# Loads given out one piece ahead, and branch B's q and k transposed by DMA, in a fused streaming-encoder layer

## The chip, the cores and the metric

The kernel runs on one core of a Trainium2 chip. The time is that of one execution on the device, in microseconds (us), as a median of several executions. Names of engines are those of the profile: PE is TensorE (PEld its weight loads), DVE is VectorE, ACT is ScalarE, POOL is GpSimd, SP is SyncE, whose queue gives out nearly all DMAs.

## The reference, cut to what matters

One layer of an encoder over 2048 prompt frames and 8 x 16 sample frames that continue running streams with 512 cached positions. All in float32; the kernel splits operands into a high and a low fp16 part and multiplies three of the four pairs.

```python
h = rms_norm(x, norm_g) * (1 + scale) + shift            # scale, shift, gate from c @ w_ada + b_ada
qa, ka, va, za, qb, kb, vb, zb, ga, gb = split(h @ w_in)  # 4*512 + 4*512 + 2*1024 columns
# branch A, 4 heads: differential attention, chunk-causal (64), after rope
w  = softmax(q1 k1^T / 8) - lam * softmax(q2 k2^T / 8);   oa = w @ va
# branch B, 8 heads: stick-breaking attention, strictly causal, no rope
z = qb kb^T / 8
a = exp(log_sigmoid(z) + reverse_cumsum(log_sigmoid(-z)) - log_sigmoid(-z));   ob = a @ vb
# merge
ya = (rms_norm(oa, subln_g) * (1 - lam_init) * silu(za)) @ w_branch_a
yb = (ob * silu(zb)) @ w_branch_b
y  = rms_norm(x + gate * ((sigmoid(ga) * ya + sigmoid(gb) * yb) @ w_out), final_g)
```

The outputs are y for prompt and samples and the new k and v of both branches.

## The kernel before, in words

The frames are cut into 17 tiles of 128: tiles 0 to 15 are the prompt, tile `NT` = 16 holds all samples. The program has three stages.

**Prologue** (lines 955 to 1182). The modulation is computed from `w_ada`, x is normalised, modulated, transposed by TensorE and kept in DRAM as `hT_d` in two fp16 halves.

**Units** (lines 891 to 1322). Eight units, each a pair of a head group and a branch: unit u has branch A for even u (`kind` 0, one head of A) and branch B for odd u (`kind` 1, two heads of B). For each unit, `project` multiplies a tile of h with 512 columns of `w_in` (24 matmuls at L438; odd units add 24 gate matmuls at L514 with their own columns). `finish` splits v, k and q into halves on ACT and DVE (`k16`, `qbuf`; L299, L304, L472, L473). `transpose_qk` then turns k (2 blocks of 128x128) and q (4 blocks) with six TensorE transposes (L527, L531) into one PSUM bank `ps_t`, the only bank of its tag, which the gate matmuls use too; two copies (L541, L542) bring them to `k` and `qst`, on ACT in A units and on DVE in B units. `scores` multiplies q with all earlier k (L649, L650, three `ps_s` banks). In A units DVE evacuates (L568) and ACT exponentiates; in B units ACT makes two sigmoids (L123), DVE scans (L626), POOL multiplies (L632), ACT casts (L582), DVE makes the low half (L583). In both, the weights are transposed by a DMA (L590, `wt`, up to 16 blocks of 128x128 each), and `pv`, two steps later (`PV_LAG`), multiplies them with v (L706 to L711).

Projections form one long list of pieces over all units, which runs some tiles ahead of the attention (`LEAD`, `take`); `interleave` mixes pieces of projection, scores and pv of one step by their costs. `transpose_qk` of a tile stands in that list five pieces after the start of the next tile's projection (`TR_AFTER`). Side work is spread over the steps: `prepare_unit` loads the next unit's 512 columns of `w_in` (and gate columns), squares them on ACT for a scale (`norm`, L281, junk output), then cuts them into halves; `norms().one` loads `w_branch`, `w_out` and the value caches and squares them likewise; the key caches go through `stages`, which already fetches one piece before it squares. Buffers of 4 KB per partition come from one list, `free`, first in, first out. The order of instructions on each engine is made by the framework's own scheduler from this program; each engine then runs its list strictly in order. On SP that means: a DMA that waits for its data holds up every DMA behind it.

**Last stage** (from L1322 on). For each tile, `inputs` loads o, z and the two gates (`g_d`, L1222), makes u = o * silu(z), takes the gates' sigmoid (L1236), squares and splits u; `turned` transposes u on TensorE (L1209); `branches` multiplies with `w_branch` (L1366) and the gates (L1368); `turned_y`, `output` (L1395) and `normed_rows` follow. `inputs` runs two tiles ahead, `turned` one tile ahead. The eight units' sample attention (`sample`, tiles `dsc`, `dks`, `dwt`) is mixed in.

## Time and profile before

| what | value |
| --- | --- |
| median of 3 executions (lowest, highest) | 2332.06 us (2321.65, 2335.35) |
| the profiled execution, its span | 2326.12 us, 2324.3 us |
| busy: PE, DVE, ACT, POOL | 2096.5, 1745.0, 1621.7, 704.5 us |
| DMA: queue of SP | 76.4% of 16 engines' span, 442 MB |
| granted PE clock, mean | 0.969 |

By stage, from the first score of a unit to that of the next (start, length): prologue 0, 134 us; unit 0 134, 183 us; unit 1 (B) 317, 233 us; unit 2 550, 194 us; unit 3 (B) 744, 241 us; unit 4 985, 188 us; unit 5 (B) 1173, 251 us; unit 6 1424, 182 us; unit 7 (B) 1606, 214 us; last stage 1820, 504 us. Tiles are numbered from 0, so tile 8 of unit 3 is the ninth prompt tile of the second B unit.

In the tables of stretches, each row gives the stretch and its length in us, then for each engine the busy time and the number of instructions, then the granted PE clock (1.00 is full), the DMA share and GB/s. In rows of groups, "x64 | 26.4, 413 | 0.0" is 64 instructions, 26.4 us busy, 413 ns each in the mean, 0.0 us idle ahead of them.

### The profile page before, as it was taken

The numbers are of one execution on the slowest core, as the hardware profiler recorded it, in microseconds if no ns is written. First come the engines' busy times: TensorE is split into PE (matmuls) and PEld (weight loads), VectorE is DVE, ScalarE is ACT, GpSimd is POOL, SyncE is SP. The second block draws the span as 40 slices with busy tenths as digits, with TensorE's granted clock in tenths as the row PEclk, the third lists the DMA queues.
The fourth block names the chain that finished last, engine by engine and source line by source line (L and its number), as shares of the span: only waits on it lengthen the run. The fifth ranks groups of instructions, "written<-read, shape, count | busy, mean of one in ns | idle before, by whom it ended". The sixth has DMA issues, their size and how long they took to land. (4 is left out here: it accounts for less than half of the span.)

```text
span 2324.3 us, 41797 instructions
## 1 busy us (share of the span) xinstructions
PE 2096.5 (90%) x14752; PEld 1123.2 (48%) x14752; DVE 1745.0 (75%) x3795; ACT 1621.7 (70%) x3228; POOL 704.5 (30%) x610
## 2 busy tenths in 40 slices
PE   5998899998989889899998998999998689899998
PEld 3654454444545445455554444555454344444443
DVE  4658668789776777997767879787778878777763
ACT  4968676788776677878676887776677666556541
POOL 1223014356410433752023346401345312122111
PEclk7999999999999999999999999999999799999999
DMA  9778558889696798878877898665667899778421
GB/s 335 272 213 212 134 146 220 198 198 184 174 239 150 201 231 186 187 184 220 183 200 206 182 221 199 171 156 138 142 157 165 191 273 256 211 219 215 143 100 52
DMA packets 805827, 445.30 MB, mean 192 GB/s; under 512 B 537354, under 2 KB 744506, under 8 KB 805104
## 3 DMA queue, kind: packets, MB, share of 16 engines
q1 hardware_dynamic: 804668, 442.24, 76.4%
q8 instruction: 115, 1.88, 0.3%
q14 instruction: 96, 0.79, 0.1%
q10 hardware_dynamic: 948, 0.39, 0.1%
HBM read 228.82 MB, written 86.02 MB: 135 GB/s over the span
## 5 line engine op out<-in xcount | busy, mean ns | idle before, releaser
L632 POOL TENSOR_TENSOR sc_p<-sc_p,sc_n 128x127 f32<-128x127 f32 (+7 forms) x192 | 311.8, 1628 | 660.2 <-DVE sc_n L626 562.8
L438 PEld LDWEIGHTS <-hs 128*128 128x128 f16 x3120 | 276.5, 99 | 263.3 <-issue 11.9
L438 PE MATMUL ps_mm<-wa,hs 128*128 128x512 f16 x1590 | 400.4, 382 | 2.9 <-DMA hs<-hT_d 2.1
L438 PE MATMUL ps_mm<-wb,hs 128*128 128x512 f16 x1530 | 394.5, 384 | 7.6 <-DMA hs<-hT_d 6.8
L626 DVE TENSOR_TENSOR_SCAN sc_n<-ps_s,sc_n,zero_t 128x512 f32<-128x512 f32 x192 | 245.4, 1278 | 72.2 <-ACT ps_s L123 67.3
L649 PE MATMUL ps_s<-k,qst 128*128 128x512 f16 (+3 forms) x640 | 226.0, 354 | 49.2 <-DVE sc_n L626 38.5
L583 DVE TENSOR_TENSOR sc_n<-sc_p,sc_n 128x128 f16<-128x128 f32 (+7 forms) x192 | 222.7, 1163 | 36.8 <-ACT sc_n L582 36.4
L514 PEld LDWEIGHTS <-hs 128*128 128x128 f16 x1632 | 156.5, 98 | 189.1 <-ACT qst L542 5.9
L123 ACT ACTIVATE sc_p<-ps_s,usc 128x512 f32<-128x512 f32 (+3 forms) x320 | 205.1, 641 | 32.5 <-PE ps_s L650 23.3
L650 PE MATMUL ps_s<-k,qst 128*128 128x512 f16 (+3 forms) x640 | 225.7, 354 | 0.0
L514 PE MATMUL ps_t<-wb,hs 128*128 128x512 f16 x918 | 216.1, 379 | 3.0 <-DVE sam L542 1.4
L710 PE MATMUL ps_o<-v,wt 128*128 128x128 f16 x1088 | 168.9, 225 | 43.1 <-DMA wt<-sc_n 42.7
L123 ACT ACTIVATE ps_s<-ps_s,usc 128x512 f32<-128x512 f32 (+3 forms) x328 | 200.5, 611 | 0.0
L582 ACT CAST sc_n<-sc_p 128x128 f16<-128x128 f32 (+7 forms) x192 | 155.2, 811 | 63.7 <-POOL sc_p L632 62.8
L1395 PE MATMUL ps_o<-wo,wb 128*128 128x512 f16 x816 | 185.2, 382 | 6.3 <-ACT wo L299 5.5
L514 PE MATMUL ps_t<-wa,hs 128*128 128x512 f16 x714 | 170.6, 381 | 6.9 <-ACT qst L542 5.7
L710 PEld LDWEIGHTS <-wt 128*128 128x128 f16 x1088 | 105.0, 101 | 104.7 <-DMA wt<-sc_n 54.6
L711 PE MATMUL ps_o<-v,wt 128*128 128x64 f16 x1088 | 154.5, 198 | 0.0
L568 DVE TENSOR_SCALAR_CACHE_REDUCE sc_n<-ps_s,usc 128x512 f32<-128x512 f32 (+3 forms) x160 | 106.2, 664 | 35.2 <-PE ps_s L650 17.2
L1366 PEld LDWEIGHTS <-wb 128*128 128x128 f16 x816 | 79.2, 100 | 105.5 <-issue 23.1
L711 PEld LDWEIGHTS <-wt 128*128 128x128 f16 x1088 | 102.9, 100 | 50.9 <-issue 2.2
L1395 PEld LDWEIGHTS <-wb 128*128 128x128 f16 x816 | 78.7, 98 | 100.4 <-issue 9.1
(370 smaller groups left out, 4515.6 us busy)
## 6 DMA issues: line engine op xcount, KB each, us to landing
hs<-hT_d SPq DMA_DIRECT2D x130, 512.0 KB, 4.6
g_d<-gt SPq DMA_DIRECT2D x68, 256.0 KB, 4.3
out_dram<-pr SPq DMA_DIRECT2D x204, 64.0 KB, 2.2
wa<-g_d SPq DMA_DIRECT2D x25, 512.0 KB, 3.8
o_d<-o SPq DMA_DIRECT2D x136, 64.0 KB, 2.6
hs<-o_d SPq DMA_DIRECT2D x17, 512.0 KB, 3.8
out_dram<-x SPq DMA_DIRECT2D x17, 512.0 KB, 2.8
wide<-in_w_ada_dram SPq DMA_DIRECT2D x8, 1024.0 KB
```

Source lines behind the costliest of these rows:

```text
L123: i = S.activation(**kw)
L438: T.matmul(box["p"], box["h"][:, hi, k, :], U["w"][k][:, wi, :], start=(n == 0), stop=(n == 3 * KT - 1))
L514: T.matmul(box["g"][:, 0:gw], box["h"][:, hi, k, :], U["wg"][k // per][:, k % per, wi, :], start=(j == 0), stop=(j == 3 * KT - 1))
L582: S.copy(out=hi, in_=src)
L583: V.tensor_tensor(out=lo, in0=src, in1=hi, op=ALU.subtract)
L626: V.tensor_tensor_scan(out=dst[:, lo : lo + n][:, ::-1], data0=src[:, 0:n][:, ::-1], data1=zero_t[:, 0:1].to_broadcast([P, n]), initial=fi ...
L632: G.tensor_tensor(out=p[:, 0:m], in0=p[:, 0:m], in1=n[:, 1 : m + 1], op=ALU.mult)
L649: T.matmul(p[:, 0:n], qst[:, c, :], kk[:, c, 0:n], start=True, stop=False)
L650: T.matmul(p[:, 0:n], qst[:, 2 + c, :], kk[:, c, 0:n], start=False, stop=not diag)
L710: T.matmul(po[:, c * P : (c + 1) * P], wt[:, wj, :], vt[:, c, :, :], start=first, stop=False)
L711: T.matmul(po[:, c * P : c * P + 64], wt[:, nb + wj, :], vt[:, c, 0, :], start=False, stop=last)
L1395: T.matmul(po, st["y"][:, yi * 8 + k, :], wo[j * 4 + k // 2][:, wi, k % 2, :], start=(n == 0), stop=(n == 3 * KT - 1))
```

## The change

Five edits.

1. `prepare_unit`: the loads of the next unit's weights and gate columns are given out one piece ahead of their squares (`staged`), in one piece more.
2. `norms().one`: the same for `w_branch`, `w_out` and the value caches.
3. Prologue: five early pieces where there were four, since unit 0's weights now have five.
4. `transpose_qk`: in B units (`kind` 1) k and q go by two DMA transposes from SP straight from `k16` and `qbuf` to `k` and `qst`. Six TensorE transposes, the PSUM bank and two DVE copies of each of their 4 x 17 tiles are gone. A units stay as they were.
5. Last stage: the gates' sigmoid leaves `inputs` for a piece of its own, `opened`, at the end of the step before its tile.

```diff
         def norm(name, k, i):
...
-            fetch(name, k)
             sum_squares(raw[name, k], 1024, U[name + "acc"][:, i : i + 1])
+
+        def staged(name, ks):
+            def piece(i):
+                if i < len(ks):
+                    fetch(name, ks[i])
+                if i > 0:
+                    norm(name, ks[i - 1], i - 1)
+            return [lambda i=i: piece(i) for i in range(len(ks) + 1)]
...
-        pieces = [lambda k=k: norm("w", k, k // 2) for k in range(0, KT, 2)] + [bounds] + [lambda k=k: cut(k) for k in range(0, KT, 2)]
+        pieces = staged("w", list(range(0, KT, 2))) + [bounds] + [lambda k=k: cut(k) for k in range(0, KT, 2)]
...
     def transpose_qk(U, t):
...
+        if U["kind"] == 1:
+            turned_to = nc.sync.dma_start_transpose
+            turned_to(out=kst, in_=k16.rearrange("p c f d -> p (c f d)"))
+            turned_to(out=qst, in_=q16.rearrange("p f c r d -> p (f c r d)"))
+        else:
+            pt = bank("t", F16)
...
-        def one(src, dst, scale):
-            st = free.pop(0)
-            free.append(st)
-            load(out=st if len(src.shape) == 2 else st.rearrange("p (j n) -> p j n", n=P), in_=src)
-            sum_squares(st, 1024, dst, scale=scale)
+        loaded = []
+
+        def one(k):
+            if loaded:
+                st, dst, scale = loaded.pop(0)
+                sum_squares(st, 1024, dst, scale=scale)
+                free.append(st)
+            if k < len(srcs):
+                src, dst, scale = srcs[k]
+                st = free.pop(0)
+                load(out=st if len(src.shape) == 2 else st.rearrange("p (j n) -> p j n", n=P), in_=src)
+                loaded.append((st, dst, scale))
...
-        for fn in early[0:4]:
+        for fn in early[0:5]:
...
-        for g in gs:
-            act(out=g, in_=g, func=AF.Sigmoid)
-
...
+    def opened(st):
+
+        for g in st["g"]:
+            act(out=g, in_=g, func=AF.Sigmoid)
...
                 work.insert(2, (0.9, lambda n=n: turned(states[tiles[n + 1]])))
+                work.append((0.1, lambda n=n: opened(states[tiles[n + 1]])))
```

The scheduler makes the lists of all engines anew. Three places show it; lines of the changed kernel are numbered up to 23 higher (L438 is L445, L590 is L602, L649 and L650 are L661 and L662, the new k and q transposes are L542 and L543).

First the list of PE at the projection of tile 9 of unit 3, at the point where the six transposes of tile 8 stood (`hs` is the projected tile's h, `wb`, `wa` the unit's weights). Before:

```order
L438 MATMUL ps_mm<-wb_1430,hs_181 128x512
L527 LDWEIGHTS k_9812
L527 MATMUL ps_t<-id_192,k_9812 128x128
L527 LDWEIGHTS k_9812
L527 MATMUL ps_t<-id_192,k_9812 128x128
L531 LDWEIGHTS qbuf_214
L531 MATMUL ps_t<-id_192,qbuf_214 128x128
L531 LDWEIGHTS qbuf_214
L531 MATMUL ps_t<-id_192,qbuf_214 128x128
L531 LDWEIGHTS qbuf_214
L531 MATMUL ps_t<-id_192,qbuf_214 128x128
L531 LDWEIGHTS qbuf_214
```

In the changed kernel, after as many projection matmuls:

```order
L445 LDWEIGHTS hs_181
L445 MATMUL ps_mm<-wa_172,hs_181 128x512
L445 LDWEIGHTS hs_181
L445 MATMUL ps_mm<-wa_172,hs_181 128x512
L445 LDWEIGHTS hs_181
L445 MATMUL ps_mm<-wa_172,hs_181 128x512
L661 LDWEIGHTS qst
L661 MATMUL ps_s<-k,qst 128x512
L662 LDWEIGHTS qst
L662 MATMUL ps_s<-k,qst 128x512
```

The transposes are gone, and the scores of tile 8 have moved up: their first matmul stood behind 1512 projection matmuls of the whole list, and now stands behind 1488.

Second the list of SP around the weights of tiles 7 and 8 of the same unit (`wt` is a transpose of weights, 16 or 2 blocks wide here; `hs` the load of h for a projection; `g_d`, `o_d` and `out` are stores, `in_cache` loads of the spread side work). Before:

```order
L590 DMA_TRANSPOSE wt<-sc_n 128x16x128 x2
L494 DMA out_dram<-pr 128x128
L495 DMA out_dram<-pr 128x128
L700 DMA o_d_68<-o 128x128
L847 DMA wb_1433<-in_cache_a_v_dram 128x8x128
L847 DMA wb_1432<-in_cache_a_v_dram 128x8x128
L590 DMA_TRANSPOSE wt<-sc_n 128x2x128
L415 DMA hs_181<-hT_d_60 128x2048
L518 DMA g_d_105<-gt_1421 128x512
L847 DMA wb_1433<-in_cache_a_v_dram 128x8x128
L847 DMA wb_1432<-in_cache_a_v_dram 128x8x128
L590 DMA_TRANSPOSE wt<-sc_n 128x16x128
```

In the changed kernel:

```order
L602 DMA_TRANSPOSE wt<-sc_n 128x16x128 x2
L602 DMA_TRANSPOSE wt<-sc_n 128x2x128
L525 DMA g_d_105<-gt_1421 128x512
L542 DMA_TRANSPOSE k<-k_9965 128x2x128
L543 DMA_TRANSPOSE qst<-qbuf_214 128x4x128
L602 DMA_TRANSPOSE wt<-sc_n 128x16x128
L602 DMA_TRANSPOSE wt<-sc_n 128x2x128
L501 DMA out_dram<-pr 128x128
L502 DMA out_dram<-pr 128x128
L712 DMA o_d_68<-o 128x128
L525 DMA g_d_106<-gt_1421 128x512
L422 DMA hs_181<-hT_d_60 128x2048
```

k and q of tile 9 now stand behind the first weights of tile 8 and ahead of the rest of them; the load of h, which stood right behind the 2-block transpose, comes nine rows later.

Third the list of ACT in the last stage, at one tile's `inputs` (`hs_181` is z, `hs_180` o, `usq` the square of u, `hs_182` u's split, `wb`, `wa` the gates, `dsc` a sample's scores, L1210 the copy of a transposed u). Before:

```order
L281 ACTIVATE junk,usq<-hs_180 128x1024
L123 ACTIVATE wb_1433<-wb_1433 128x1024
L1372 CAST wa_173<-wa_171 128x512
L299 ACTIVATE hs_182<-hs_180,suy 128x1024
L123 ACTIVATE wa_171<-wa_171 128x1024
```

In the changed kernel:

```order
L281 ACTIVATE junk,usq<-hs_180 128x1024
L123 ACTIVATE hs_181<-hs_181 128x512
L123 ACTIVATE wb_1426<-wb_1426 128x1024
L299 ACTIVATE hs_182<-hs_180,suy 128x1024
L1229 COPY wa_171<-ps_s 128x1024
L123 ACTIVATE wb_1429<-wb_1429 128x1024
```

The two sigmoids on gates still stand near the split of u, but they belong to a tile whose gates were loaded a step earlier.

More of the change, by code (lines that the diff above doesn't have):

```diff
@@ L539, in transpose_qk @@
             kst = U["k"][g][:, :, i * P : (i + 1) * P]
-        copy = V.tensor_copy if U["kind"] == 1 else S.copy
-        copy(out=kst, in_=pt[:, 0:256].rearrange("p (c n) -> p c n", c=2))
-        copy(out=qst, in_=pt[:, 256:768].rearrange("p (j n) -> p j n", j=4))
+        if U["kind"] == 1:
[4 more added lines that the diff above has]
+            pt = bank("t", F16)
+            for c in range(2):
+                T.transpose(pt[:, c * P : (c + 1) * P], k16[:, c, :, :].rearrange("p f d -> p (f d)"), id16)
+            for f in range(2):
+                for c in range(2):
+                    j = 2 + f * 2 + c
+                    T.transpose(pt[:, j * P : (j + 1) * P], q16[:, f, c, :, :].rearrange("p r d -> p (r d)"), id16)
+            copy = V.tensor_copy if U["kind"] == 1 else S.copy
+            copy(out=kst, in_=pt[:, 0:256].rearrange("p (c n) -> p c n", c=2))
+            copy(out=qst, in_=pt[:, 256:768].rearrange("p (j n) -> p j n", j=4))
         if t == NT:
@@ L1285, in first @@
                 turned(states[t])
+                opened(states[t])
         def rest():
```

13 lines of the change are left out of this document (3 added, 10 removed).

## The prediction

> **What bounds the kernel now.** I read the page's first part, then the stretches by stage, then the waits.
>
> ```profile
> PE 2096.5 (90%) x14752; PEld 1123.2 (48%) x14752; DVE 1745.0 (75%) x3795; ACT 1621.7 (70%) x3228; POOL 704.5 (30%) x610
> ...
> 550.00:744.00 194.00, 181.03 (x1308) 100.05 (x1309) 150.95 (x407) 144.38 (x322) 51.95 (x53) 0.99 0.81 191
> 744.00:985.00 241.00, 217.29 (x1501) 114.98 (x1499) 188.35 (x309) 185.08 (x382) 108.00 (x84) 0.98 0.85 200
> ...
> 1606.00:1820.00 214.00, 192.14 (x1362) 102.97 (x1360) 172.88 (x273) 160.09 (x321) 90.77 (x66) 0.96 0.69 153
> 1820.00:2324.00 504.00, 444.64 (x3166) 218.79 (x3164) 353.26 (x788) 267.38 (x366) 97.62 (x67) 0.95 0.69 186
> ```
>
> PE is busy 90 to 93% of every stage of units, DVE and ACT about 78% in unit 3 (744 to 985). An average hides two kinds of stretch:
>
> ```profile
> 784.00:804.00 20.00, 15.28 (x74) 7.15 (x72) 12.65 (x28) 10.27 (x23) 7.41 (x7) 0.74 0.73 191
> 964.00:984.00 20.00, 17.39 (x163) 10.38 (x163) 19.72 (x23) 17.77 (x34) 14.80 (x12) 1.00 0.83 179
> 1666.00:1686.00 20.00, 20.00 (x134) 10.32 (x133) 12.93 (x18) 14.20 (x28) 5.66 (x4) 1.00 0.70 152
> ```
>
> The middle of a B unit is PE's own (20.00 of 20.00); its last tiles are DVE's (19.72). The first row is what a stall does: PE waits, the granted clock falls to 0.74, and 74 matmuls start where the third row has 134. The waits behind it:
>
> ```profile
> PE ps_o L710 <- DMA wt<-sc_n: 42.7, 29, 4.9
> PE ps_s L649 <- DVE sc_n L626: 38.5, 45, 3.4
> ...
> PE ps_o L706 <- DMA wt<-sc_n: 20.8, 19, 2.6
> ...
> PE ps_s L1209 <- DVE dsc L626: 17.7, 5, 5.7
> ```
>
> Each is a late link of the same chain: PE's scores, ACT's sigmoids, DVE's scan (which frees the `ps_s` bank), POOL's product, and the weights that a DMA transposes for pv. L710 is pv of B units, L706 of A units, the last row the samples in the last stage.
>
> **The change part by part.** All sums stand against the profiled execution, 2326.1 us (span 2324.3), which is 5.9 below the median of 2332.1.
>
> *Six transposes off PE.* In an A unit, where the same six stand, PE's rows are:
>
> ```profile
> 599.83 0.28 PE L527 MATMUL ps_t<-id,k 128*128 128x128 f16 x2
> 599.95 0.39 PE L531 MATMUL ps_t<-id,qbuf 128*128 128x128 f16 x4
> 600.17 0.59 PE L438 MATMUL ps_mm<-wa,hs 128*128 128x512 f16 x2
> ```
>
> Durations overlap, so starts count: 600.17 - 599.83 = 0.34 us for six. In B units there are 4 x 17 = 68 tiles: 68 x 0.34 = 23 us. All these transposes come before the DVE stretches at the units' ends, nearly all where PE is the limit: I take -20 (bounds -23 and 0, the latter if other chains end there).
>
> *Waits in front of them.*
>
> ```profile
> L527 PE MATMUL ps_t<-id,k 128*128 128x128 f16 x272 | 38.3, 222 | 17.5 <-DVE k L304 9.0 <-ACT qst L542 4.8 <-ACT gt L517 3.6
> L514 PE MATMUL ps_t<-wb,hs 128*128 128x512 f16 x918 | 216.1, 379 | 3.0 <-DVE sam L542 1.4 <-DVE qst L542 1.0 <-DVE csc L867 0.5
> L514 PE MATMUL ps_t<-wa,hs 128*128 128x512 f16 x714 | 170.6, 381 | 6.9 <-ACT qst L542 5.7 <-DVE sam L542 1.2
> ```
>
> Of the 17.5 us the parts released by `k L304` and by ACT's `qst` are A units' and stay. What goes with B's use of `ps_t`: 3.6 (gate copy) + 1.4 + 1.0 + 1.2 = 7.2 us. I take -6 (0 to -7).
>
> *DVE's copies.*
>
> ```profile
> L542 DVE COPY qst<-ps_t 128x512 f16<-128x512 f16 x64 | 26.4, 413 | 0.0
> L541 DVE COPY k<-ps_t 128x256 f16<-128x256 f16 x64 | 17.7, 276 | 5.8 <-PE ps_t L531 5.7
> ```
>
> 0.69 us a tile, 47 us in all off DVE. It pays only where PE waits for the scan (38.5 us above), mostly at the units' ends, where no copies stood. -3 (0 to -10).
>
> *Loads ahead of their squares.*
>
> ```profile
> L281 ACT ACTIVATE junk<-wa 128x1024 f16<-128x1024 f32 x68 | 72.0, 1059 | 45.7 <-DMA wa<-in_x_prompt_dram 11.1 <-DMA wa<-in_cache_b_k_dram 9.1 <-DMA wa<-in_w_in_dram 7.0
> L281 ACT ACTIVATE junk<-wb 128x1024 f16<-128x1024 f32 x56 | 59.4, 1061 | 39.6 <-DMA wb<-in_w_in_dram 13.8 <-DMA wb<-in_cache_a_v_dram 11.0 <-PE ps_s L220 5.1
> ```
>
> ACT stands up to 85 us ahead of squares; x and the key caches were not changed, so some 50 go. ACT's sigmoids feed the scan, so a few of the 38.5 us of PE's waits end sooner: -5 (0 to -15). The five early prologue pieces do the four's work; the first 79 rows of SP's list are unchanged: 0.
>
> *Gates' sigmoid.*
>
> ```profile
> L123 ACT ACTIVATE wa<-wa 128x1024 f32<-128x1024 f32 x25 | 26.3, 1056 | 50.0 <-DMA wa<-g_d 50.0
> ...
> 601.44 4.05 PE L438 MATMUL ps_mm<-wb,hs 128*128 128x512 f16 x18
> ```
>
> ACT loses 50.0 us to `g_d` at these 25 sigmoids alone. But in the last stage it is busy only 267 of 504 us, and the largest piece of PE's 59 idle ones is the 17.7 behind the samples' scans. A shorter ACT queue feeds those scans earlier: -4 (0 to -15). If a late `opened` put two sigmoids of 1.06 us ahead of L1368, the cover is two `ps_mm` groups of 12 matmuls at 4.05 / 18 = 0.22 us, over 5 us; without it, 2 us for each of 17 tiles.
>
> *What it adds: 136 DMA transposes on SP.* Nothing of 2 or 4 blocks from `k16` exists; the nearest are the weights' transposes, of 2 to 16 blocks.
>
> ```profile
> L590 SPq DMA_TRANSPOSE wt<-sc_n x288: 1167/1746/5657, 147.3 to 1830.6; - x144
> ...
> DMA to landing us min/median/max: 2.3/4.3/6.8
> ```
>
> The smallest issue takes 1.17 us. At 1.2, two a tile are 2.4, and 136 are 163 us of SP's time. How full is SP? The first and last of its 167 issues in unit 3's stretch:
>
> ```profile
> 743.94 0.38 SPq L700 DMA_DIRECT2D o_d<-o  x1
> ...
> 984.66 3.36 SPq L590 DMA_TRANSPOSE wt<-sc_n  x1
> ```
>
> They add up to 160 of 241 us; 34 more at 1.2 make 201, or 83%. The DMA engines stand at 0.85 in that stage; its 102 added blocks of 32 KB are 3.3 MB, which at the row's 200 GB/s is 17 us of 241, 0.07 more: in the mean not full. Queued behind each new issue, and behind its wait for DVE, is everything else on SP: h for the next projection, the weights for pv, the stores that free `pr` and `gt`. PE's waits on these stand at 42.7 us (L710) and, for h,
>
> ```profile
> L438 PE MATMUL ps_mm<-wb,hs 128*128 128x512 f16 x1530 | 394.5, 384 | 7.6 <-DMA hs<-hT_d 6.8
> ```
>
> If lateness grew by half, that is 49.5 / 2 = +25. Weights have two steps until pv and h one tile, most of it slack, so I take +6 (0 to +25), nearer the end at which slack holds.
>
> *q later for its scores.* In SP's list of front, q of tile 9 stands behind the 2-block weights of tile 8. In the trace these and the first score of tile 9 are, for units 3 and 5:
>
> ```profile
> 848.30 1.45 SPq L590 DMA_TRANSPOSE wt<-sc_n  x1
> ...
> 857.06 0.27 PE L649 MATMUL ps_s<-k,qst 128*128 128x256 f16 x1
> ...
> 1279.97 6.95 SPq L590 DMA_TRANSPOSE wt<-sc_n  x2
> ...
> 1288.68 0.27 PE L649 MATMUL ps_s<-k,qst 128*128 128x256 f16 x1
> ```
>
> The weights' issue ends at 849.75; k takes 1.2, q lands 2.3 to 4.3 after its start: 853.3 to 855.3, against 857.06. In unit 5: 1286.92 + 1.2 + 2.3 to 4.3 = 1290.4 to 1292.4, against 1288.68, so 2 to 4 us late. The lists also bring such scores forward: 24 projection matmuls less stand ahead of tile 8, at 0.22 us some 5 us of cover. I count two such places in each of the four B units (tiles 9 and 10, in unit 7 tiles 4 and 5) at 1.3 us, between nothing and the 4 us just found: +10 (0 to +32). Scores are not alone behind it: the next projection's matmuls wait on PE too.
>
> Sum: -20 - 6 - 3 - 5 - 4 + 6 + 10 = **-22 us**, to 2304 against the profiled execution; against the median, 2310.
>
> [...] PE's rows give 0.34 / 6 = 57 ns a block, and the two issues that replace a tile's six blocks take SP 2.4 us. [...]
>
> **The rivals.**
>
> *SP's line becomes the bound of the B units (slower).* k and q wait at the head of SP for DVE, weights and h pile up behind, and PE stands at first scores long enough to lose its clock. For it: 83% of SP's time in issue alone, which leaves 40 us a unit for every wait at SP's head. Against: in the middle of unit 7 the DMAs are lighter (0.70) and PE is full. Price: the stretch at 784 falls 60 matmuls short of 134, 60 / 134 x 20 = 9 us. Two more like it in each of four units are 72 us; less the gains of 38 that is +34, 2366 against the median. It decides once q's landing slips some 4 us beyond my count. [...]
>
> *PE does not get the time.* The scan ends each wait anyway: `ps_s` <- L626 grows by what the transposes leave. For it: DVE and ACT at 78% of unit 3 with only 10% of PE left. Against: 20.00 of 20.00 at 1666. Gains of 38 shrink to 16 and are eaten by +16: 2332.
>
> *SP's slack covers all.* Nothing of the +16, and the squares and gates pay at the far ends: -23 - 7 - 6 - 12 - 12 = -60: 2272.
>
> **How the numbers follow.** About 1% (23 us) is what a measurement can tell from no change here, since the three executions spread over 0.6%. My forecast, -8 to -45, has 0.45, of which 0.25 is beyond 1% faster; the full gain 0.2; PE not getting it 0.1; SP as the bound 0.25, all of it beyond 1% slower in the sum. So faster 0.45, same 0.30, slower 0.25. The range leaves out the outer half of the full gain and of SP as the bound: 2268 to 2366. The forecast's own is 2287 to 2324.
>
> **What would show it.** Right: no L527 or L531 in B units, PE's instructions down by 408, busy PE down in 317 to 1820; ACT's waits at L281 for `in_w_in` and `in_cache` and at the gates near nothing. Wrong: `L661 <- DMA qst` or `k` of over 15 us in total; `wt` and `hs` waits over 1.5 times; stretches with a clock under 0.9 in units 1, 3, 5. If the B units' stretches are as long as before with PE idle at the scan, the second rival holds. What could break the forecast is SP's lateness, which I took from slacks of the old order.

## The result, and the profile after

The changed kernel takes 2334.6 us (median of 20; 2329.6 to 2339.6) where the kernel before takes 2329.0 (20 executions; 2321.7 to 2335.5). The ratio is 1.0017, 95% interval 1.0007 to 1.0026: some 4 us slower, nothing a reader would call a change. The forecast was 2310 us, 22 us faster; the time lies in the stated range of 2268 to 2366, but outside that of the likeliest case, 2287 to 2324, and on the other side of no change.

First the profile's first part for the changed kernel, and the answer on span and clock.

```profile
PE 2089.3 (90%) x14344; PEld 1111.3 (48%) x14344; DVE 1695.3 (73%) x3659; ACT 1618.7 (69%) x3228; POOL 693.9 (30%) x610
```

```profile
core 0: 2330.4 us, clock 0.961
```

PE has 408 matmuls less, as forecast, and DVE 50 us less. Yet PE's busy time fell by only 7.2 us (2096.5 to 2089.3). Three numbers of these rows add up to the span, and the rest of this section reads every kernel by them: **idle** is span less PE's busy time; **clock loss** is (1 - granted clock) x span, the time that PE would have saved at full clock if it had been busy throughout (in the changed kernel two score matmuls start 0.21 us apart at 980.88, at clock 1.00, and 0.41 us apart at 982.62, at 0.50); **work** is busy time less clock loss.

| kernel | span | idle | clock loss | work |
| --- | --- | --- | --- | --- |
| before | 2324.3 | 227.8 | 72.1 | 2024.4 |
| changed | 2330.4 | 241.1 | 90.9 | 1998.4 |
| difference | +6.1 | +13.3 | +18.8 | -26.0 |

So the transposes' time did go: 26 us of PE's work. It was given back as 13 us of standing still and 19 us of running at a lower clock. The mean clock is given in steps of 0.001, so each loss is good to about 1 us.

Two cautions go with this table. PE stands idle for a part of the slow stretches; counted over its busy time alone, the clock costs 49 and 68 us and the work is 2047 and 2021 us, the same 26 apart. Counted like that, the work of all kernels below falls into two groups, 2043 to 2047 us with six TensorE transposes a tile and 2020 to 2027 without (e13_actq, 2032, and e18_k_act, which keeps four of six, 2037, aside). And these are single executions: over all of them the mean clock is 0.963 for the changed kernel (0.957 to 0.967) and 0.967 to 0.968 for the kernel before, which makes the clock's part some 11 us, not 19.

Where it stands still, from the chain of waits of the changed kernel (engine, tile and line waiting; what for; us in all, times, longest):

```profile
PE ps_s L661 <- DVE sc_n L638: 57.5, 54, 3.3
PE ps_o L722 <- DMA wt<-sc_n: 37.8, 23, 4.8
PE ps_o L718 <- DMA wt<-sc_n: 22.4, 18, 2.6
PE ps_s L1228 <- DVE dsc L638: 11.5, 2, 6.7
PE ps_mm L445 <- DMA hs<-hT_d: 11.2, 5, 3.7
```

Against 38.5, 42.7, 20.8 and 17.7 us before, in the rows of the prediction, and for h

```profile
PE ps_mm L438 <- DMA hs<-hT_d: 9.0, 5, 3.0
```

The waits that SP's lateness was expected to raise, weights and h, are as they were (71.4 against 72.5 together). The wait for the scan rose by 19 us. And the same stretches as in the prediction, with the last one to the longer span's end:

```profile
744.00:985.00 241.00, 212.92 (x1429) 111.23 (x1428) 180.96 (x288) 189.62 (x395) 105.36 (x84) 0.99 0.91 209
...
1606.00:1820.00 214.00, 191.79 (x1307) 101.55 (x1305) 169.44 (x252) 164.81 (x331) 90.98 (x66) 0.94 0.78 166
1820.00:2330.00 510.00, 448.46 (x3164) 221.20 (x3162) 343.60 (x787) 267.44 (x366) 92.10 (x67) 0.94 0.70 184
```

In unit 3 and unit 7 PE starts 72 and 55 matmuls fewer in the same time, where 102 transposes a unit are gone, and is busy 4.4 and 0.4 us less. DVE is lighter by 7 and 3 us there and ACT fuller by 5. The units end where they ended before: the last score ends at 1816.6 us, against 1816.7. The 6 us that the profiled execution is longer lie in the last stage, 513.8 us against 507.6 from there on, and it transposes no k or q. That stage is no steady ground: with the same 3172 matmuls in all twenty kernels of this text it takes 500 to 517 us. SP's new issues are (duration of one in ns: smallest, median, largest)

```profile
L542 SPq DMA_TRANSPOSE k<-k x64: 1167/1176/2411, 252.6 to 1771.7; - x64
```

```profile
L543 SPq DMA_TRANSPOSE qst<-qbuf x64: 1188/1217/3183, 259.2 to 1773.0; - x64
```

just the 1.2 us that was taken from the weights' transposes. Last, the squares and the gates' sigmoids on ACT:

```profile
L281 ACT ACTIVATE junk<-wa 128x1024 f16<-128x1024 f32 x72 | 76.7, 1066 | 46.5 <-DMA wa<-in_cache_a_k_dram 12.4 <-DMA wa<-in_x_prompt_dram 10.6 <-DMA wa<-in_cache_a_v_dram 8.6
L281 ACT ACTIVATE junk<-wb 128x1024 f16<-128x1024 f32 x52 | 55.2, 1062 | 31.8 <-DMA wb<-in_w_in_dram 12.5 <-DMA wb<-in_cache_b_v_dram 12.2 <-DMA wb<-in_w_out_dram 3.0
...
L123 ACT ACTIVATE wb<-wb 128x1024 f32<-128x1024 f32 x34 | 34.4, 1049 | 9.5 <-DMA wb<-g_d 9.5
```

The gates' waits went, from 65 us, the 50.0 of the prediction's row and the 15.4 of this one, to 10:

```profile
L123 ACT ACTIVATE wb<-wb 128x1024 f32<-128x1024 f32 x9 | 9.5, 1059 | 15.4 <-DMA wb<-g_d 15.4
```

The squares' did not: 85 us before, 78 now. Although their loads are written one piece ahead, they wait as long.

One place shows how this looks. In unit 3, tile 13, the changed kernel has

```profile
917.54 1.53 SPq L331 DMA_DIRECT2D wb<-in_w_in_dram  x2
919.17 3.61 SPq L602 DMA_TRANSPOSE wt<-sc_n  x1
...
924.74 1.06 ACT L281 ACTIVATE junk<-wb 128x1024 f16<-128x1024 f32 x1 [2.83 <-DMA wb<-in_w_in_dram]
...
927.92 1.28 DVE L638 TENSOR_TENSOR_SCAN sc_n<-ps_s,sc_n,zero_t 128x512 f32<-128x512 f32 x1 [0.78 <-ACT ps_s L123]
...
929.26 0.38 PE L661 MATMUL ps_s<-k,qst 128*128 128x512 f16 x1 [3.29 <-DVE sc_n L638]
```

SP issues from 905 to 940 with hardly a gap. ACT stands 2.83 us at a square whose two loads were issued from 917.54 on and landed at 923.2 and 924.6; the sigmoids come behind the square, DVE's scan behind these, and PE stands 3.29 us for the bank that the scan frees. At the same tile before, PE's waits for scans are 0.7 us in all. That gave the first theory. The place itself does not decide it: the loads were on their way some 3 us before ACT came to the square, so what it stood for there is the rest of a transfer of over 5 us. Whether that was late in SP's list or slow in the DMA engines this place does not tell; the loads of this form take 3.9 to 4.0 us in the median of the kernel before.

### The profile page after: what moved, and what is told of

Its sections match the earlier page's. It is cut to its first block, busy times and chain, and to the rows that moved or that the text cites. A ratio compares the mean times of both kernels' runs of the same rounds, so it can differ in the third digit from the quotient of the medians.

```text
span 2330.4 us, 41287 instructions
## 1 busy us (share of the span) xinstructions
PE 2089.3 (90%) x14344; PEld 1111.3 (48%) x14344; DVE 1695.3 (73%) x3659; ACT 1618.7 (69%) x3228; POOL 693.9 (30%) x610
## 5 line engine op out<-in xcount | busy, mean ns | idle before, releaser
L445 PE MATMUL ps_mm<-wb,hs 128*128 128x512 f16 x1734 | 448.6, 385 | 4.6 <-DMA hs<-hT_d 4.6
L445 PEld LDWEIGHTS <-hs 128*128 128x128 f16 x3120 | 275.7, 99 | 263.6 <-DMA hs<-hT_d 12.7
L445 PE MATMUL ps_mm<-wa,hs 128*128 128x512 f16 x1386 | 349.0, 380 | 6.6 <-DMA hs<-hT_d 6.6
L661 PE MATMUL ps_s<-k,qst 128*128 128x512 f16 (+3 forms) x640 | 228.3, 357 | 72.3 <-DVE sc_n L638 57.5
L595 DVE TENSOR_TENSOR sc_n<-sc_p,sc_n 128x128 f16<-128x128 f32 (+7 forms) x192 | 205.7, 1076 | 49.9 <-ACT sc_n L594 49.6
L521 PE MATMUL ps_t<-wb,hs 128*128 128x512 f16 x918 | 232.4, 380 | 0.0
L662 PE MATMUL ps_s<-k,qst 128*128 128x512 f16 (+3 forms) x640 | 228.0, 357 | 0.0
L722 PE MATMUL ps_o<-v,wt 128*128 128x128 f16 x1088 | 193.6, 228 | 37.9 <-DMA wt<-sc_n 37.8
L521 PEld LDWEIGHTS <-hs 128*128 128x128 f16 x1632 | 144.5, 99 | 140.5 <-issue 10.1
L521 PE MATMUL ps_t<-wa,hs 128*128 128x512 f16 x714 | 187.7, 391 | 6.8 <-ACT qst L554 6.0
L1417 PE MATMUL ps_o<-wo,wa 128*128 128x512 f16 x816 | 182.8, 380 | 2.1 <-ACT wo L299 1.3
L723 PE MATMUL ps_o<-v,wt 128*128 128x64 f16 x1088 | 174.9, 200 | 0.0
L580 DVE TENSOR_SCALAR_CACHE_REDUCE sc_p<-ps_s,usc 128x512 f32<-128x512 f32 (+3 forms) x160 | 106.2, 664 | 26.4 <-PE ps_s L662 24.3
L718 PE MATMUL ps_o<-v,wt 128*128 128x128 f16 x544 | 105.0, 225 | 22.8 <-DMA wt<-sc_n 22.4
```

Source lines behind the costliest of these rows:

```text
L445: T.matmul(box["p"], box["h"][:, hi, k, :], U["w"][k][:, wi, :], start=(n == 0), stop=(n == 3 * KT - 1))
L521: T.matmul(box["g"][:, 0:gw], box["h"][:, hi, k, :], U["wg"][k // per][:, k % per, wi, :], start=(j == 0), stop=(j == 3 * KT - 1))
L580: V.tensor_scalar(out=dst[:, lo : lo + n], in0=p[:, 0:n], scalar1=sc_pos, scalar2=None, op0=ALU.mult, op1=ALU.max, accum_out=job["mx"][:, ...
L595: V.tensor_tensor(out=lo, in0=src, in1=hi, op=ALU.subtract)
L661: T.matmul(p[:, 0:n], qst[:, c, :], kk[:, c, 0:n], start=True, stop=False)
L662: T.matmul(p[:, 0:n], qst[:, 2 + c, :], kk[:, c, 0:n], start=False, stop=not diag)
```

## The experiments

**Theory A (the line).** SP's list is nearly full; the 136 new issues delay what stands behind them, and PE gets the delay over several chains. **Theory B.** PE does not get the time: the chain of scans ends its waits anyway, whatever the transposes cost. Further rivals came up on the way: the transfers' traffic, and k and q that arrive late. In the later expectations theory A stands as L, against D, the transfers. All ratios are to the kernel before on the same chip; differences between two kernels are differences of their ratios times 2330 us, with the two intervals combined.

### Which edit: e1_turn, e2_noturn, e11_gates

The kernel before with edit 4 alone:

```diff
-        pt = bank("t", F16)
-        ... six T.transpose, two copies
+        if U["kind"] == 1: two nc.sync.dma_start_transpose (as in the change)
+        else: as before
```

> The kernel before with edit 4 alone (k and q of B units turned by DMA), loads and gates as before. Theory A, SP's line: the 136 issues delay the loads of weight columns, ACT's squares stand behind these loads, and sigmoids, scans and scores behind the squares; without the staged loads this is worse than in the changed kernel: 10 to 25 us slower than before, ACT's waits at L281 in the units above 90 us. Theory B, PE does not get the time: the scans end PE's waits however the transposes are made, and SP is not to blame: within 5 us of before.

Measured: 1.0075 (1.0055 to 1.0096), 17 us slower, as theory A had it. Its sign at the squares is missed: they wait 76 us in the units, not above 90.

The changed kernel without edit 4:

```diff
-        if U["kind"] == 1: two nc.sync.dma_start_transpose
-        else:
+        (all units) six T.transpose into ps_t, two copies
```

> The changed kernel without edit 4 (TensorE transposes and DVE copies as before; loads, prologue and gates as changed). Theory A: 8 to 20 us faster than before, since the loads now come ahead of their squares; ACT's waits for DMA at the squares in the units fall from 70 to under 35 us. Theory B: edits 1, 2, 3 and 5 are worth next to nothing or cost what the changed kernel lost: between 0 and 6 us slower than before.

Measured: 0.9972 (0.9956 to 0.9988), 6 us faster. Its squares wait 42 us for DMAs in the units, where before has 69 and the changed kernel 67. Theory A had 8 to 20 us and waits of under 35 us, so both fall short of it.

The kernel before with edit 5 alone:

```diff
-        for g in gs:
-            act(out=g, in_=g, func=AF.Sigmoid)
+    def opened(st): ...            # called at the end of the step before
```

> The kernel before with edit 5 alone (the gates' sigmoid in a piece of its own at the end of the step before). As predicted: 4 us faster, the 50 us of ACT's waits for the gates near nothing. If the last stage is bound elsewhere, 0 and within 2 us; edits 1 to 3 then carry the 6 us that e2_noturn gained.

Measured: 1.0002 (0.9988 to 1.0015). ACT's waits for the gates are gone, as this group shows (25 sigmoids; 50.0 us idle before them in the kernel before), and the time has not moved:

```profile
L123 ACT ACTIVATE wa<-wa 128x1024 f32<-128x1024 f32 x25 | 25.6, 1049 | 6.7 <-DMA wa<-g_d 6.7
```

So, by difference, edits 1 to 3 carry the 6 us (+-4); edit 5 is worth nothing (+-3); edit 4 costs 17 us (+-5) without the staged loads and 10 us (+-4) with them (1.0017 less 0.9972). That staging is worth more when SP is fuller would fit, but the two hardly differ by more than their intervals.

### What PE's part is worth: e3_unturned, e4_both

The changed kernel with no transposes of either kind in B units:

```diff
-            turned_to(out=kst, in_=k16.rearrange("p c f d -> p (c f d)"))
-            turned_to(out=qst, in_=q16.rearrange("p f c r d -> p (f c r d)"))
+            V.tensor_copy(out=kst, in_=k16.rearrange("p c f d -> p c (f d)"))
+            V.tensor_copy(out=qst, in_=q16.rearrange("p f c r d -> p (f c) (r d)"))
```

> The changed kernel with neither kind of transpose in B units: two DVE copies bring k16 and qbuf to k and qst as they are, so the transposition of k and q of branch B is left out. PE, SP and DMAs are all free of it. Theory A: with SP free too, PE's 23 us are had: 20 to 40 us faster than before. Theory B: within 6 us of the changed kernel (2329 to 2341), PE's waits for the scan L638 at 55 us or more.

Measured: 0.9931 (0.9912 to 0.9950), 16 us faster than before. So B in its pure form falls: with SP out of the way PE does get something. But theory A's 20 to 40 us are not reached either. Counted over PE's busy time, it has 26 us less work than e2_noturn (2020 against 2046), and it is only 10 us faster (+-6; 5.5 us in the profiled executions): there the clock costs 70 us where e2_noturn has 56, and PE is idle for 227.5 us against 220.8.

The changed kernel with the six TensorE transposes kept beside the DMAs, unread:

```diff
+        pt = bank("t", F16)
+        six T.transpose, in all units
         if U["kind"] == 1:
             two DMA transposes
```

> The changed kernel with the six TensorE transposes kept beside the DMAs in B units, their result in PSUM unread: PE has the work of before, SP that of after. Theory A: PE's transposes cost what they cost before, since PE has no idle time to spare: 10 to 25 us slower than the changed kernel. Theory B: within 5 us of the changed kernel, PE's waits for scans shrinking by what the transposes fill.

Measured: 1.0141 (1.0121 to 1.0160), 29 us slower than the changed kernel (+-5), a little more than theory A's 10 to 25. Here PE's transposes and their waits for `ps_t` are worth what they were sized at, 26 us, with SP's part the same on both sides. And e4_both against e2_noturn, which differ by the DMAs in place of DVE's copies, is 39 us (+-6): that is the other side of the account. Against copies (e3_unturned to the changed kernel) the DMA transposes cost 20 us (+-5). So the same 10 us between e2_noturn and the changed kernel can be read as 10 gained and 20 lost, by way of e3_unturned, or as 39 lost and 29 gained, by way of e4_both; which kernel stands in the middle decides.

### Through what: e5_line, e6_plain, e9_bytes, e16_unread

All four are e3_unturned with something added or put in place of the copies, so they have PE's shorter list in common. Like e3_unturned they leave the transposition of branch B's k and q out of what is computed (e16_unread for the prompt only). Six tiny DMAs on SP a tile:

```diff
+            for j in range(3):
+                load(out=tick[0:1, j, 0:32], in_=k16[0:1, j % 2, j // 2, 0:32])
+            for j in range(3):
+                load(out=tick[0:1, 3 + j, 0:32], in_=q16[0:1, j % 2, j // 2, 0, 0:32])
```

> The kernel of e3_unturned (k16 and qbuf copied by DVE, the transposition of branch B's q and k left out) with six tiny DMAs of 64 bytes a tile on SP, which wait for the same k16 and qbuf: some 2.4 us of SP's line a tile and no traffic. Theory L, the line: SP's time and its waits at the head are what the DMA transposes cost, so most of the 20 us between e3_unturned and the changed kernel come back: 10 to 20 us slower than e3_unturned, 2325 to 2340 on a chip where before takes 2333. Theory D, the transfers: their 3.3 MB a unit in 256-byte packets slow the other DMAs, and SP's line is slack: within 5 us of e3_unturned.

Measured: 0.9966 (0.9949 to 0.9982), 8 us slower than e3_unturned (+-6): less than theory L has for the whole price, more than D's nothing.

Plain DMAs in place of the copies:

```diff
-            two V.tensor_copy
+            load(out=kst, in_=k16.rearrange("p c f d -> p c (f d)"))
+            for j in range(2):
+                load(out=qst[:, j::2, :], in_=q16.rearrange("p f c r d -> p (f c) (r d)")[:, j::2, :])
```

> The same, but k and q go by three plain DMAs a tile in 256-byte pieces from k16 and qbuf to k and qst, without DVE copies: the packets and the arrival of the changed kernel, but a shorter issue (some 0.4 us each) and no transposing; the transposition is left out. Theory L: a third to a half of SP's time, so 3 to 10 us slower than e3_unturned. Theory D by bytes: like the changed kernel, 15 to 22 us slower than e3_unturned; by the transposing itself: within 5 us of e3_unturned.

Measured: 0.9999 (0.9984 to 1.0014), 16 us slower than e3_unturned (+-6). That is more than theory L's 3 to 10 us and fits traffic, or data arriving late.

The same traffic, with nobody waiting for it:

```diff
             two V.tensor_copy
+            load(out=spill[:, 0:2, 0:P], in_=k16.rearrange("p c f d -> p c (f d)"))
+            load(out=spill[:, 2:6, 0:P], in_=q16.rearrange("p f c r d -> p (f c) (r d)"))
```

> The kernel of e3_unturned (transposition of branch B's q and k left out) with two plain DMAs a tile from k16 and qbuf to a scratch in DRAM, in the same 768 pieces of 256 bytes that the transposes move, and nobody waits for them. Some 65 us of SP's issue, the whole traffic, no late q or k. Theory L, the line: 4 to 9 us slower than e3_unturned, 0.3 to 0.5 percent faster than before. Theory D, the transfers: 15 to 20 us slower than e3_unturned, within 0.15 percent of before. If q and k arriving late were the price in e6_plain, this comes out below e6_plain by 8 us or more.

Measured: 0.9927 (0.9906 to 0.9948), the time of e3_unturned. Theory D's 15 to 20 us are missed, and so are the 4 to 9 that theory L had for the issues. Traffic costs nothing here, though it ends in DRAM and not in the buffers of k and q, and by this row of its stretches (unit 3) there was plenty: 0.96 of the DMA engines, more than the changed kernel's 0.91.

```profile
744.00:985.00 241.00, 219.16 (x1466) 114.49 (x1465) 194.05 (x314) 191.87 (x397) 112.31 (x88) 0.97 0.96 211
```

The real DMA transposes, unread:

```diff
+            if t < NT:
+                two V.tensor_copy to kst and qst
+                unread = stg.tile([P, 6, P], F16, tag="sam", ...)
+                qst, kst = unread[:, 0:4, :], unread[:, 4:6, :]
             turned_to(out=kst, ...)
             turned_to(out=qst, ...)
```

> The changed kernel's DMA transposes, 136 with the same sources and waits on SP, but for the prompt tiles into a buffer that nobody reads; k and qst come from DVE copies as in e3_unturned (the transposition of branch B's prompt q and k is left out). SP's line and the transfers are those of the changed kernel, and no score waits for a DMA. If the 20 us between e3_unturned and the changed kernel are the line's (what stands behind on SP): 15 us or more slower than e3_unturned, at most 0.05 percent faster than before. If they are the late k and q: within 5 us of e3_unturned, 0.5 to 0.7 percent faster than before. A part each: between.

Measured: 1.0018 (1.0005 to 1.0030): the time of the changed kernel to the digit, though no score of the prompt waits for a DMA. So late k and q are not the price, unless DVE's copies, which e16_unread has and the changed kernel has not, cost as much by chance. PE's waits for scans are 65.8 us, for weights 69.6 and for h 13.0 (first fence), where e3_unturned has 46.3, 66.2 and 4.4 (second fence).

```profile
PE ps_s L666 <- DVE sc_n L643: 65.8, 53, 4.5
PE ps_o L727 <- DMA wt<-sc_n: 41.9, 24, 4.9
PE ps_o L723 <- DMA wt<-sc_n: 27.7, 19, 5.0
PE ps_mm L445 <- DMA hs<-hT_d: 13.0, 5, 3.3
```

```profile
PE ps_s L660 <- DVE sc_n L637: 46.3, 42, 4.8
PE ps_o L721 <- DMA wt<-sc_n: 41.7, 21, 4.0
PE ps_o L717 <- DMA wt<-sc_n: 24.5, 18, 3.4
...
PE ps_mm L445 <- DMA hs<-hT_d: 4.4, 2, 2.7
```

What these four kernels, e3_unturned and the changed one have on SP in the stretches of the B units (939 us together), summed over its rows in the trace: the time of all issues, and the time that SP stood at the head of its list waiting for data or buffers.

| kernel | issues | issue us | waiting at the head us | slower than e3_unturned |
| --- | --- | --- | --- | --- |
| e3_unturned | 623 | 635 | 262 | - |
| e9_bytes | 722 | 711 | 175 | -1 |
| e5_line | 905 | 717 | 152 | +8 |
| e6_plain | 756 | 736 | 151 | +16 |
| e16_unread | 710 | 755 | 128 | +20 |
| changed | 714 | 758 | 132 | +20 |

Taken as SP's slack, the wait at the head orders these kernels: 76 us more of issue cost nothing while 175 us of slack were left; the next 45 us cost 20. That is what theory A has for a queue that fills. It is not shown to be the whole price. e5_line and e6_plain have the same slack and differ by 8 us, and e9_bytes has hardly less issue time than e5_line and does not pay. The table cannot part issue time from something in the transposing itself, since the last two kernels have both; e5_line and e6_plain have no transposing and pay too. And of what the profiled executions of the changed kernel and of e16_unread are longer than e3_unturned's (13 and 23 us), 8 and 11 us lie behind the last score, where no k or q is transposed.

### Over which chain: e10_deep

The loads of weight columns two pieces ahead of their squares:

```diff
-                if i > 0:
-                    norm(name, ks[i - 1], i - 1)
+                if i > 1:
+                    norm(name, ks[i - 2], i - 2)
```

> The changed kernel with the weights' and gate columns' loads two pieces ahead of their squares where there was one. If SP's lateness reaches PE through ACT's squares (their waits for DMA in the units are 66 us, against 42 in e2_noturn), these waits fall and the kernel is 5 to 12 us faster than the changed one. If the squares are beside the path: within 3 us of the changed kernel.

Measured: 0.9992 (0.9979 to 1.0006), 6 us faster than the changed kernel (+-4). But the squares' waits in the units did not fall (77 us against 67). And e3_unturned and e9_bytes stand 62 and 65 us at squares without paying. So the time is in the range that was expected of the squares, without the fall of their waits that should bring it. The stall at 929 is real, but squares are not **the** chain; PE stands longer in several places (from e3_unturned to e16_unread scans +20 us, h +9, weights +3, together the idle time's +31; clock loss -11 in the profiled executions, 0 in the mean of all), and no single one is shown to carry the price.

### SP relieved: e7_act, e8_noturn_act, e15_free_act, e13_actq

The changed kernel with 204 stores, whose sources ACT has just written, given out by ACT:

```diff
+            store_by = load if kind == 0 else S.dma_start
-            load(out=out_rows(nk, t, h * P, P), in_=rot[:, 128:256])
-            load(out=out_rows(nv, t, h * P, P), in_=pr[:, 256:384])
+            store_by(out=out_rows(nk, t, h * P, P), in_=rot[:, 128:256])
+            store_by(out=out_rows(nv, t, h * P, P), in_=pr[:, 256:384])
...
-                load(out=g_d[t][:, g0 : g0 + gw], in_=gt[:, 0:gw])
+                S.dma_start(out=g_d[t][:, g0 : g0 + gw], in_=gt[:, 0:gw])
```

> The changed kernel with 204 stores given out by ACT instead of SP: B units' new k and v rows from pr, and all gates from gt, whose sources ACT has just written. SP has some 90 us of issue less. Theory L: SP's line is relieved by half of what the transposes added: 5 to 12 us faster than the changed kernel, unless ACT's issues cost as much. Theory D: the traffic is the same: within 4 us of the changed kernel, or slower by ACT's issue time.

Measured: 0.9939 (0.9920 to 0.9958), 18 us faster than the changed kernel (+-5), more than theory L's 5 to 12, and faster than the kernel before by 14. SP's slack in the B units is 180 us again.

The same stores in e2_noturn:

> The kernel of e2_noturn with the same 204 stores given out by ACT. Theory L: SP's line was a limit before too (ACT's squares still wait 42 us for loads): 3 to 8 us faster than e2_noturn, 10 to 15 us faster than before. Theory D: within 3 us of e2_noturn, or slower by ACT's issue time.

Measured: 0.9937 (0.9906 to 0.9968), 8 us faster than e2_noturn (+-8), so hardly clear of nothing, and level with e7_act.

The same stores in e3_unturned:

> The kernel of e3_unturned (transposition of branch B's q and k left out) with the 204 stores given out by ACT: no transposes on SP, and SP relieved. If relief by the stores takes away the price of the DMA transposes, this is within 5 us of e7_act (0.6 percent faster than before). If the transposes still cost their price there, this is 12 to 20 us faster than e7_act (1.1 to 1.5 percent faster than before).

Measured: 0.9889 (0.9875 to 0.9904). The DMA transposes' price, 20 us before, is 12 us (+-6) when the stores are off SP: lower, not gone. e7_act has 180 us of slack and pays these 12, where e9_bytes with 175 paid nothing, so the fill of SP's list does not explain all of it.

The 136 transposes on ACT's queue:

```diff
-            turned_to = nc.sync.dma_start_transpose
+            turned_to = S.dma_start_transpose
```

> The changed kernel with the 136 DMA transposes of k and q given out by ACT's queue: the same transfers, SP's line as short as before. ACT's queue must wait for DVE's low halves before each. Theory L: 10 to 20 us faster than the changed kernel, as far as ACT's own waits leave it. Theory D: no faster than the changed kernel, and slower by what ACT stands at the head for DVE, up to 68 times 2 us.

Measured: 1.1020 (1.0999 to 1.1041), 240 us slower. ACT's sequencer waits ahead of many of the transposes, up to 7.7 us, and the instructions behind it with it (the group of these waits at L542, ns; then an ACT cast that nothing but its queue held up):

```profile
L542 ACTq EVENT_SEMAPHORE  x112: 17/38/7679, 235.9 to 2012.3; - x112
```

```profile
923.55 1.18 ACTq L542 DMA_TRANSPOSE k<-k  x1
924.78 0.94 ACT L594 CAST sc_n<-sc_p 128x896 f16<-128x896 f32 x1 [2.90 <-issue]
```

The trace tells what these waits are for. Of some 197 us at L542 and L543, 188 are ended by the landing of a weights' transpose that SP gave out. SP in turn stands for ACT's transposes ahead of its own, 364 us in all (the two largest rows):

```profile
SPq L602 <- DMA qst<-qbuf: 169.9, 45, 7.3
SPq L602 <- DMA k<-k: 163.6, 41, 6.6
```

In the changed kernel, with all transposes on SP, SP's waits have no such row. So in e13_actq the transposes of the two queues wait for each other, on both sides, and neither theory had that. The run says nothing on SP's line; it shows what waits on ACT's own queue and on SP's cost together.

### Further relief: e12_more, e14_more, e17_deep_act, e18_k_act

210 more stores of A units (v rows, z, o) on ACT, in e8_noturn_act and in e7_act:

```diff
...
-                load(out=z_d[t][:, ui : ui + P], in_=pr[:, 384:512])
+                S.dma_start(out=z_d[t][:, ui : ui + P], in_=pr[:, 384:512])
...
-        load(out=o_d[t][:, ui : ui + P], in_=o)
+        (S.dma_start if U["kind"] == 0 else load)(out=o_d[t][:, ui : ui + P], in_=o)
```

> The kernel of e8_noturn_act with A units' v rows, z and o given out by ACT too (some 210 more stores whose sources ACT has written). If SP's line still holds something up in A units: 2 to 6 us faster than e8_noturn_act, 0.7 to 0.9 percent faster than before. If not: within 2 us of it.

> The same stores on ACT in the changed kernel with its DMA transposes. If the transposes' price is SP's line and enough of it is free now, PE's 25 us come through: 8 us or more faster than e12_more. If PE gets no more than the clock and the chain of scans leave: within 5 us of e12_more.

Measured: 1.0086 (1.0069 to 1.0103) and 1.0013 (1.0001 to 1.0025). The first is 35 us slower than e8_noturn_act, where 2 to 6 us faster or no change was expected; the second is 17 us slower than e7_act, nearly all that the first 204 stores had gained. Between them the DMA transposes are 17 us faster (+-5), as theory A has it for a line with room (in the B units SP issues for 501 us in the first), but the pair is slow for a reason that was not settled.

Loads two pieces ahead as in e10_deep, in e8_noturn_act; and k alone by DMA, q by TensorE, in e7_act:

```diff
+        if B:
+            nc.sync.dma_start_transpose(out=kst, in_=k16.rearrange("p c f d -> p (c f d)"))
+        else: two T.transpose of k
         four T.transpose of q
```

> The kernel of e8_noturn_act (TensorE transposes, 204 stores on ACT) with the weights' loads two pieces ahead of their squares as in e10_deep. If the waits at the squares (41 us) still reach PE: 2 to 6 us faster than e8_noturn_act, 0.7 to 0.9 percent faster than before. If not: within 2 us of it.

> The kernel of e7_act (204 stores on ACT) with k alone by DMA and q's four blocks by TensorE again: half the added issues on SP, a third of PE's 25 us. If the price grows steeply as SP fills, half the issues cost little (0 to 3 us) and 8 us of PE come through: 0.7 to 0.95 percent faster than before. If each issue costs the same: within 0.15 percent of e7_act and e8_noturn_act (0.5 to 0.75 percent faster).

Measured: 1.0044 (1.0031 to 1.0058) and 1.0011 (0.9997 to 1.0025): 25 and 17 us slower than the kernels that they were made from. No theory here has that: SP's slack in the B units is 382 and 287 us. In e17_deep_act the loads of h come late, eight of its ten waits in unit 7; SP itself stands ahead of them for the gate matmuls (L522), which free the buffer. SP's and PE's rows of it:

```profile
SPq L422 <- PE ps_t L522: 84.7, 24, 9.2
```

```profile
PE ps_mm L445 <- DMA hs<-hT_d: 14.7, 10, 3.1
```

e8_noturn_act has 0.1 us there, e18_k_act 16.3 and e12_more 15.0. Each edit makes the scheduler write new lists for all engines, and the kernels differ by as much as the effects under study. That the lists are the cause is argued from these rows, not shown. It puts a bound on the readings above: a single pair of kernels proves little, whether it differs by 10 us or by 20.

What carries more weight is that many kernels agree. PE's idle time between the first score and the last, in the profiled executions, is 132 to 142 us in the seven kernels with neither DMA transposes of k and q nor e5_line's or e6_plain's DMAs (before, e2_noturn, e3_unturned, e8_noturn_act, e9_bytes, e11_gates, e15_free_act). It is 150 to 165 us in six of the seven that have all of the DMA transposes on SP (changed, e1_turn, e4_both, e10_deep, e14_more, e16_unread); the seventh, e7_act, has 145, near e6_plain and e5_line with 146 and 149. Against this stand e12_more and e17_deep_act, with 156 and 152 and no DMA transposes of k and q at all. So it takes more than one pair of kernels to say that these transposes on SP cost PE idle time, and most of them say so; that the fill of SP's list alone does it is not shown.

Of the kernels that compute everything none beats e7_act and e8_noturn_act: 14 us faster than before, with either kind of transposes.

## Why the prediction was wrong, point by point

- **Six transposes off PE, -20; waits for `ps_t`, -6; DVE's copies, -3.** Right in size as work: -26 us by the accounts. As time it is less sure. With SP's part held equal (e4_both to the changed kernel) the transposes and their waits are worth the -29 us. With SP free of transposes (e2_noturn to e3_unturned) 26 us less work gained 10: in the profiled executions 14 us of it went to a lower clock and 7 to more idle time. So "-20, nearly all where PE is the limit" took the work for time. The granted clock stood in the rows that the prediction quoted (0.74 at 784), and it priced the clock only in a rival. DVE's copies were not run by themselves. PE's busy share, quoted as 90 to 93% of every stage of units, is 89 to 96% by the rows.
- **Loads ahead, -5.** Together with the gates 6 us, by difference all of it from the loads: right in size. The mechanism was half right: without edit 4 the squares' waits in the units fall from 69 to 42 us, with the DMA transposes on SP they stay at 67.
- **Gates' sigmoid, -4.** Nothing. 50 us of ACT's waits went and freed no one: in the last stage ACT is idle for half the time, as the prediction itself had noted.
- **136 transposes on SP, +6 (0 to +25).** This is the step that failed. The issue time was right (1.2 us each; 201 us of unit 3's 241 were forecast, the trace has 196). The choice "nearer the end at which slack holds" was wrong: the price is 20 us against DVE's copies with PE free of the transposes, and 39 with PE's transposes kept (e2_noturn to e4_both). It was weighed by PE's waits for weights and h, since those stand behind the new issues, but these did not rise together (72.5 to 71.4). What rose are the waits for scans, 38.5 to 57.5 us, and the clock's loss; the path from SP's list to these is not shown. The number to ask for was SP's own: 288 us of waiting at its head in 939 us, of which 158 us more of issue left 132. Two of the signs that the prediction set up for SP's lateness did not tell it: q's waits were to pass 15 us and are 4.2, those for weights and h were to grow by half and did not grow together.
- **q late for its scores, +10.** Nothing that can be seen: PE waited 4.2 us for q, and e16_unread, in which no score of the prompt waits for a DMA, takes the same time.
- **The rivals.** SP's line as the bound named the right place: the added issues on SP do cost. But its path, first scores that stand for k and q and weights and h that pile up, is not what the rows show, and its size is off: 72 us in four units were forecast, 20 to 39 came. "PE does not get the time" gave the right time (2332) with its sign, scan waits up from 38.5 to 57.5 us; but e3_unturned shows that PE does get part of it once SP is free, so its number is in part luck.

So the sum was -38 + 16; measured, by way of e4_both, -29 for PE's transposes and their waits (e4_both to the changed kernel), -6 for the loads, 0 for the gates, and +39 for the DMAs on SP in place of DVE's copies (e2_noturn to e4_both): +4. By way of e3_unturned it is -10, -6, 0 and +20.

## What to carry to other kernels

Before work is moved to a DMA queue, sum that queue's issue time and its waiting at the head for the stage in question: the first is its load, the second its slack, and here a price appeared while 128 to 152 us of slack were left. What PE saves is worth less than its length when PE stands still more often for it or runs at a lower clock (from e2_noturn to e3_unturned 26 us less work gained 10 us, with 14 us more of clock loss and 7 more of idle time in the profiled executions); read work, idle and clock loss apart. And where a scheduler rewrites all lists for each edit, hold the other edits equal and use several kernels before a difference of 10 or 20 us is given a cause.

## What was not expected of the hardware

In e7_act ACT's queue gave out plain DMAs while ACT computed. Here the 0.37 us of the store lie within the 1.06 us of the square:

```profile
759.67 1.06 ACT L281 ACTIVATE junk<-wa 128x1024 f16<-128x1024 f32 x1
...
759.76 0.37 ACTq L503 DMA_DIRECT2D out_dram<-pr  x1
```

204 of them, 81 us of issue, left ACT's busy time at 1621.9 us (1618.7 in the changed kernel). e13_actq, where the queue had to wait, is the other side.

In the profiled executions the granted clock fell to one half 22 times before and 29 times in the changed kernel; 13 and 14 of these stretches lasted 3.41 us, 4 and 11 of them 6.83, the longest 23.89. The length of a stall alone does not tell whether a fall follows. In the changed kernel the 3.29 us at 926 left the clock whole; a stall of 2.57 us that ended at 980.9 was followed by 6.8 us at half. The stall at 926 lies across the first two stretches below, in which PE is busy for 1.78 of 3.42 and 1.76 of 3.41 us; the later one lies within the third, ahead of the fall, in which PE is busy for 1.33 us. What decides between the two is not shown (start and length, busy times, clock, DMA; the last row is what follows):

```profile
924.19:927.61 3.42, 1.78 (x12) 0.89 (x11) 0.35 (x1) 2.87 (x7) 0.00 (x0) 1.00 1.47 234
927.61:931.02 3.41, 1.76 (x13) 0.93 (x13) 1.82 (x2) 2.62 (x6) 0.00 (x0) 1.00 0.74 178
978.80:982.21 3.41, 1.33 (x15) 0.86 (x15) 3.31 (x4) 3.41 (x7) 0.00 (x0) 1.00 0.71 133
```

```profile
982.00:989.00 7.00, 6.25 (x59) 4.57 (x57) 6.97 (x9) 4.21 (x8) 5.56 (x5) 0.51 0.74 166
```
